# A DiT block on one core: the first modulation with the weight blocks stationary and the two condition columns moving

## The chip, the cores and the metric

The kernel runs on one core of a Trainium2 chip. The core has five engines that run side by side: TensorE (PE in the rows; its weight loads are listed apart as PEld), VectorE (DVE), ScalarE (ACT), GpSimd (POOL) and SyncE (SP, which here only issues transfers). The metric is the device time of one execution in microseconds (us); lower is better.

## What is computed

One block of a hybrid transformer: 2048 tokens of width 1024, 256 context tokens, everything in fp32. What matters here is the start, cut from the reference:

```python
mod   = silu(c)     @ w_ada + b_ada          # w_ada: 1024 x 6144
mod_c = silu(c_ctx) @ w_ada + b_ada
sh1, sc1, g1, sh2, sc2, g2 = split(mod, 6)   # six pieces of 1024
csh1, csc1, ... = split(mod_c, 6)
hx = rmsnorm(x, norm1)   * (1 + sc1)  + sh1
hc = rmsnorm(ctx, norm1) * (1 + csc1) + csh1
# then: hx and hc through w_in, gated linear attention in chunks, pooling, w_out,
# a SwiGLU with w_up and w_down, and a last norm
```

The change concerns `silu(c) @ w_ada` and `silu(c_ctx) @ w_ada` for the first two of the six pieces (columns 0 to 2047 of `w_ada`), which give `sh1`, `sc1`, `csh1` and `csc1`. Two vectors of 1024 are multiplied with a matrix of 1024 x 2048.

## The kernel before

The kernel is one function. The order of the instructions on each engine is set by a scheduler that runs over the whole program before it is built, with pools of buffers as constraints; a change in one stage can therefore move instructions in a later one. fp32 products are mostly made of three fast ones: a number is split into a rounded part in a faster fp32 format (fp32r; ScalarE copies, line 147) and the rest (VectorE subtracts, line 150), and the products high x high, high x low and low x high are summed in PSUM.

The first stage, lines 358 to 419, makes the modulation in four groups g, and does the context rows in the same loop. A group stands for 256 of the 1024 columns of `sh1` and the same of `sc1`. In a group:

- Eight blocks of `w_ada` (128 rows x 512 columns, tile `wada`, 256 KB, 12 buffers) are loaded by SP (line 365). Behind the eighth, SP loads a piece of `w_in` for the value projection (tile `xt`, line 388).
- For six of the eight, ScalarE makes the rounded part `adh` and VectorE the rest `adl` (line 373). Both are moving operands, 512 columns, of a matmul whose stationary operand is the small tile `sc4`, 128 x 4: the high and the low part of the columns c and c_ctx (lines 374 and 375). For the last two blocks, fp32 itself is the moving operand (line 369, stationary `scz`, 128 x 4).
- The result is a tile of 4 rows x 512 columns in PSUM. ScalarE copies it out (`mrow`, line 391), TensorE turns it into columns with four transposes (line 394), VectorE copies and adds the halves (`mod`, lines 396 and 397), and three short VectorE instructions make `B1` and `A1`, shift and scale by column (lines 402 to 405).
- Then `turn` gives the normed context rows, transposed by line 289, their scale and shift (`hb`, line 298 on ScalarE and 296 on VectorE), the result is split into `qh` and `ql`, the piece of `w_in` into `wvh` and `wvl` (line 407; its low part on GpSimd for the first three groups, on VectorE for the last), and 24 matmuls of 264 columns (lines 323 to 325, called from 413) add the group's share of the context's values and gates. These 24 are called the value block below.

After the four groups come the first pair of row tiles of x (transposes of line 289 again, 16 in all), the context's keys (lines 508 to 510) and then pair after pair of x.

Of the kernel before, what the change touches and what calls it, by code (L numbers as in the profile page):

```python
# [8 lines left out]
F32 = mybir.dt.float32  # L9
F32R = mybir.dt.float32r  # L10
BF16 = mybir.dt.bfloat16
AF = mybir.ActivationFunctionType
ALU = mybir.AluOpType
# [8 lines left out]
def tile_hybrid_block(ctx: ExitStack, tc: tile.TileContext, x, c, cx, c_ctx, w_ada, b_ada, norm1, w_in, conv_qk,  # L22
                      gate_bias, pool_w, pool_scale, head_norm, w_out, norm2, w_up, w_down, norm_f, out):
    nc = tc.nc
    P = 128
    T, D = x.shape[1], x.shape[2]
    TC = cx.shape[1]
    KD = D // P
# [11 lines left out]
    def pool(name, bufs=1, side="left"):  # L40
        return tc.tile_pool(name=name, bufs=bufs, side=side, reuse_waits="tile")

    def psum(name, bufs):
        return tc.tile_pool(name=name, bufs=bufs, space=PSUM, reuse_waits="tile")

    def r32(ap):
        return ap.bitcast(F32)
# [3 lines left out]
    const = cst.enter_context(tc.tile_pool(name="const", bufs=1))  # L51
# [3 lines left out]
    ident = const.tile([P, P], F32, name="ident")  # L55
# [9 lines left out]
    gbias = const.tile([P, 16], F32, name="gbias")  # L65

    scv = const.tile([P, 2, KD], F32, name="scv")
    sc4 = const.tile([P, KD, 4], F32R, name="sc4")

    scz = const.tile([P, KD, 4], F32, name="scz")  # L70
    nc.vector.memset(scz.rearrange("p k w -> p (k w)"), 0.0)
    keep = ExitStack()
    rwp = keep.enter_context(pool("rw", 3))
    vtp = keep.enter_context(pool("vt", 4))
# [2 lines left out]
    gps = pfs.enter_context(psum("gps", 1))  # L77
    tp = p1.enter_context(psum("tp", 3))
# [7 lines left out]
    pv = gps.tile([P, 512], F32, name="gps")  # L86
    nc.tensor.transpose(out=pv[:, :16], in_=crow, identity=ident[:16, :16])
    nc.vector.tensor_copy(scv.rearrange("p w k -> p (w k)"), pv[:, :16])
    scp = scv.rearrange("p w k -> p k w")
    nc.vector.tensor_copy(sc4[:, :, 0:2], scp)  # L90
    nc.vector.tensor_copy(scz[:, :, 0:2], scp)
    nc.vector.tensor_tensor(sc4[:, :, 2:4], scp, sc4[:, :, 0:2].bitcast(F32), op=ALU.subtract)

    def small_vectors():
        rows = early.tile([P, P], F32, name="rows")
        for o, n, src in ((C_BADA, 48, b_ada), (C_N1, 8, norm1), (C_N2, 8, norm2), (C_PS, 4, pool_scale),
                          (C_HN, 4, head_norm)):
            nc.scalar.dma_start(rows[o:o + n], src.rearrange("o (k p) -> (o k) p", p=P))
        nc.scalar.dma_start(rows[C_CV:C_CV + 12], conv_qk.rearrange("j (k p) -> (j k) p", p=P))
        nc.scalar.dma_start(gbias, gate_bias.to_broadcast([P, 16]))  # L100
        pv = gps.tile([P, 512], F32, name="gps")
        nc.tensor.transpose(out=pv[:, :NV], in_=rows[:NV, :], identity=ident[:NV, :NV])
        nc.vector.tensor_copy(vecs, pv[:, :NV])
# [41 lines left out]
    def split(src, hi, lo, eng_hi, eng_lo):  # L145
        if eng_hi is nc.scalar:
            nc.scalar.copy(hi, src)  # L147
        else:
            eng_hi.tensor_copy(hi, src)
        eng_lo.tensor_tensor(lo, src, r32(hi), op=ALU.subtract)  # L150
# [116 lines left out]
    def load_rows(sm, xp, src, rows):  # L267

        xs = []
        ss = sm.tile([P, 2], F32, name="ss")  # L270
        for i, r in enumerate(rows):
            xt = xp.tile([P, D], F32, name="xt")
            nc.scalar.dma_start(xt, src[r * P:(r + 1) * P, :])
            jk = sm.tile([P, D], BF16, name="jk", bufs=1)
            nc.scalar.activation(jk, xt, AF.Square, accum_out=ss[:, i:i + 1])
            xs.append(xt)
        rs = rstd_of(sm, ss, D, 2, "n")
        for i in range(2):
            nc.vector.tensor_scalar(xs[i], xs[i], rs[:, i:i + 1], None, op0=ALU.mult)
        return xs  # L280
# [54 lines left out]
    def v_store(dst, vst):  # L335
        nc.sync.dma_start(dst, vst.rearrange("p h v -> p (h v)"))

    def v_tile():
        vst = sm.tile([P, 4, 129], F32, name="vst", bufs=2)
        nc.gpsimd.memset(vst[:, :, 128:129], 1.0)  # L340
        return vst
# [16 lines left out]
    with pool("adap", 4, "right") as ap_:  # L358
        xc, turned = None, None
        for g in range(4):  # L360
            ks = range(2 * g, 2 * g + 2)
            pm = tp.tile([P, 512], F32, name="tp")[0:4, :]
            for k in range(KD):
                wt = ap_.tile([P, 512], F32, name="wada", bufs=12)
                w_last = nc.sync.dma_start(wt.rearrange("p (s c) -> p s c", s=2),
                                           w_ada[k * P:(k + 1) * P, 0:2 * D].rearrange("p (s c) -> p s c", s=2)
                                           [:, :, g * 256:(g + 1) * 256])
                if k in (6, 7):
                    nc.tensor.matmul(pm, lhsT=scz[:, k, :], rhs=wt, start=False, stop=(k == KD - 1))
                else:  # L370
                    wh = ap_.tile([P, 512], F32R, name="adh", bufs=6)
                    wl = ap_.tile([P, 512], F32R, name="adl", bufs=6)
                    split(wt, wh, wl, nc.scalar, nc.vector)
                    nc.tensor.matmul(pm, lhsT=sc4[:, k, :], rhs=wh, start=(k == 0), stop=False)
                    nc.tensor.matmul(pm, lhsT=sc4[:, k, :], rhs=wl, start=False, stop=(k == KD - 1))
                if g == 0 and k == 1:
                    small_vectors()
                    wgs = sm.tile([P, KD, 2, 8], F32, name="wgs", bufs=1)
                    nc.scalar.dma_start(wgs.rearrange("p k b g -> p k (b g)"),
                                        w_in[:, O_G:O_G + 16].rearrange("(k p) c -> p k c", p=P))  # L380
                if g == 0 and k == 3:
                    xc = load_rows(sm, xp, cx, (0, 1))
                    turned = turn(tp, "tp", xc, *hbs, A1[:, 1], B1[:, 1])
            if g == 0:
                split(wgs, wvh[:, :, :, 256:264], wvl[:, :, :, 256:264], nc.vector, nc.vector)
            st = xp.tile([P, D], F32, name="xt")
            with tc.issue_after(w_last.ins):
                nc.sync.dma_start(st.rearrange("p (k c) -> p k c", k=2),
                                  w_in[ks[0] * P:(ks[1] + 1) * P, O_V:O_V + 512].rearrange("(k p) c -> p k c", p=P))
            mrow = ap_.tile([4, 512], F32, name="mrow", bufs=2)  # L390
            nc.scalar.copy(mrow, pm)
            pt = gps.tile([P, 512], F32, name="gps")
            for m in range(4):
                nc.tensor.transpose(out=pt[:, 4 * m:4 * m + 4], in_=mrow[:, m * P:(m + 1) * P], identity=ident[0:4, 0:4])
            mod = ap_.tile([P, 4, 4], F32, name="mod", bufs=2)
            nc.vector.tensor_copy(mod.rearrange("p m w -> p (m w)"), pt[:, :16])
            nc.vector.tensor_tensor(mod[:, :, 0:2], mod[:, :, 0:2], mod[:, :, 2:4], op=ALU.add)
            kk = slice(ks[0], ks[1] + 1)

            def col(o):  # L400
                return vecs[:, None, o + ks[0]:o + ks[1] + 1].to_broadcast([P, 2, 2])
            nc.vector.tensor_tensor(B1[:, :, kk], mod[:, 0:2, 0:2].rearrange("p k w -> p w k"), col(C_BADA), op=ALU.add)
            nc.vector.tensor_tensor(A1[:, :, kk], mod[:, 2:4, 0:2].rearrange("p k w -> p w k"), col(C_BADA + 8),
                                    op=ALU.add)
            nc.vector.scalar_tensor_tensor(A1[:, :, kk], A1[:, :, kk], 1.0, col(C_N1), op0=ALU.add, op1=ALU.mult)
            next(turned)
            split(st.rearrange("p (k b c) -> p k b c", k=2, b=2), wvh[:, kk, :, 0:256], wvl[:, kk, :, 0:256],
                  nc.scalar, nc.gpsimd if g < 3 else nc.vector)
            src = hbs[g // 2][:, :, 2 * (g % 2):2 * (g % 2) + 2].rearrange("p e k c -> p k e c")
            split(src, qc[0][:, kk], qc[1][:, kk], nc.scalar, nc.vector)  # L410
            for i in range(NCC):
                for b in range(2):
                    v_mm(lambda k, e: (qc[0][:, k, e], qc[1][:, k, e]), i, b, pvs[i][b], ks)
        for i in range(NCC):
            vst = v_tile()
            for b in range(2):
                v_out(vst, b, pvs[i][b], cgat[:, i])
            v_store(s_vc[i * P:(i + 1) * P, :], vst)
# [273 lines left out]
    tp = tpp.enter_context(psum("tp1", 2))  # L692
# [474 lines left out]
    for t in range(NCH + 2):  # L1167
# [4 lines left out]
        m = t - 3  # L1172
        norm = second_norm(order[m] // 2, [X_.pop(m), X_.pop(m - 1)]) if m >= 0 and m % 2 else iter(())
        m = t - 2
# [8 lines left out]
        m = t - 1  # L1183
# [42 lines left out]
    with ExitStack() as pr:  # L1226
# [50 lines left out]
        for half in range(2):  # L1277
# [3 lines left out]
            for ff in range(NF):  # L1281
                m, fh = divmod(ff, 2)
# [9 lines left out]
                g = [tmp.tile([P, 512], F32, name=f"g{n}", bufs=2) for n in range(2)]  # L1292
# [237 lines left out]
```

## Time and profile before

| | us |
|---|---|
| time before, median of three runs | 2144.59 |
| lowest and highest of the three | 2134.82, 2145.74 |
| the profiled execution, its own time | 2133.75 |
| its span in the trace | 2132.0 |
| PE busy in the span | 2022.3 (95%) |
| DVE busy | 1411.3 (66%) |
| ACT busy | 903.2 (42%) |
| POOL busy | 231.5 (11%) |

The trace counts microseconds from the start of the span. A share of busy time is an average over the whole program; the stage of the change takes some 57 of the 2132 us, and what counts there is read from the rows of that stage. A matmul's own duration contains a fixed latency, so the rate at which TensorE works is read from the distance of the starts. An fp32 matmul whose operands are not in the faster format is listed as two rows (two passes, each with its own weight load).

### The profile page before, as it was taken

What the parts mean: (1) busy time and instruction counts of PE and PEld (TensorE: products, weight loads), DVE (VectorE), ACT (ScalarE), POOL (GpSimd) and SP (SyncE); (2) the same over time, 40 slices, a digit from 0 to 9 for tenths busy, and PEclk for the clock granted to TensorE, in tenths of its full rate; (3) what the DMA queues carried; (4) which work ended last, traced back from release to release, by engine and by line L of the source; (5) the groups of instructions that cost most, each with busy time, mean ns of one, the idle gap of its engine ahead of it and who ended that gap; (6) DMA issues with size and microseconds to landing.
All of it is one profiled execution on the core that took longest, in us unless ns stands there. A gap on an engine that the chain in (4) does not pass through costs nothing.

```text
span 2132.0 us, 27467 instructions
## 1 busy us (share of the span) xinstructions
PE 2022.3 (95%) x9482; PEld 1641.3 (77%) x9482; DVE 1411.3 (66%) x2398; ACT 903.2 (42%) x1792; POOL 231.5 (11%) x222
## 2 busy tenths in 40 slices
PE   7989999995899998999999999999999999999998
PEld 3988776674687776788888877888888788888887
DVE  6866889877365656766676578776777554447664
ACT  5644644455344544433333344333333344433442
POOL 1000123210333320000000000000000002004121
PEclk9999999996899999999999999999999999999999
DMA  8597666568477775434343267556655584644642
GB/s 278 162 291 230 204 229 197 161 184 231 136 219 238 213 220 176 148 97 147 100 141 112 96 199 249 187 188 203 188 186 194 177 325 141 221 148 157 229 162 99
DMA packets 355059, 397.80 MB, mean 187 GB/s; under 512 B 22388, under 2 KB 243160, under 8 KB 354152
## 3 DMA queue, kind: packets, MB, share of 16 engines
q1 hardware_dynamic: 308976, 324.62, 47.5%
q10 hardware_dynamic: 45944, 71.43, 10.3%
q8 instruction: 74, 1.21, 0.2%
q14 instruction: 65, 0.53, 0.1%
HBM read 269.44 MB, written 126.54 MB: 186 GB/s over the span
## 4 chain that ended last, share of the span: by engine, by line
PE 73%; DMA 11%; DVE 8%; issue 3%; ACT 3%; SPq 1%; POOL 1%; ACTq 0%; DVEq 0%; POOLq 0%
PE pa L619 8%; PE pa L620 8%; PE pa L621 8%; PE pdn L1356 7%; PE pdn L1358 7%; PE pdn L1357 7%; PE pg L619 4%; PE pg L621 4%; PE pg L620 4%; PE pb L619 2%; PE pb L621 2%; PE pb L620 2%; DMA hst<-s_hb 2%; PE pm L1138 2%; PE pm L1140 1%
## 5 line engine op out<-in xcount | busy, mean ns | idle before, releaser
L619 PE MATMUL pa<-h,wh 128*128 128x512 f32 x680 | 271.5, 400 | 8.1 <-ACT p L633 4.6
L621 PE MATMUL pa<-h,wl 128*128 128x512 f32 x680 | 270.6, 399 | 0.0
L620 PE MATMUL pa<-h,wh 128*128 128x512 f32 x680 | 270.4, 398 | 0.0
L147 ACT CAST wh<-ws 128x512 fp32r<-128x512 f32 x224 | 138.3, 620 | 299.1 <-PE pg L620 160.7
L1356 PE MATMUL pdn<-ow,op 128*128 128x512 f32 x616 | 236.8, 389 | 1.0 <-ACT op L147 1.0
L1357 PE MATMUL pdn<-ow,op 128*128 128x512 f32 x616 | 237.5, 389 | 0.0
L1358 PE MATMUL pdn<-ow,op 128*128 128x512 f32 x616 | 237.5, 389 | 0.0
L150 DVE TENSOR_TENSOR op<-ra,op 128x512 fp32r<-128x512 f32 x154 | 121.3, 794 | 156.3 <-ACT op L147 156.1
L150 DVE TENSOR_TENSOR wl<-ws,wh 128x512 fp32r<-128x512 f32 x224 | 156.7, 702 | 56.9 <-ACT wh L147 56.6
L147 ACT CAST op<-ra 128x512 fp32r<-128x512 f32 x154 | 95.2, 621 | 222.5 <-PE pdn L1358 220.0
L620 PE MATMUL pg<-h,wh 128*128 128x512 f32 x448 | 177.9, 397 | 2.4 <-DVE h L150 2.4
L619 PE MATMUL pg<-h,wh 128*128 128x512 f32 x448 | 177.5, 397 | 1.4 <-ACT h L147 1.4
L621 PE MATMUL pg<-h,wl 128*128 128x512 f32 x448 | 177.5, 396 | 1.1 <-DVE wl L150 1.1
L619 PEld LDWEIGHTS pa<-h,wh 128*128 128x128 f32 x680 | 128.9, 190 | 43.4 <-ACT p L633 6.4
L621 PEld LDWEIGHTS pa<-h,wl 128*128 128x128 f32 x680 | 128.9, 190 | 31.0 <-issue 1.2
L620 PEld LDWEIGHTS pa<-h,wh 128*128 128x128 f32 x680 | 128.9, 190 | 29.9 <-issue 0.5
L593 DVE TENSOR_TENSOR ws<-raw 128x512 f32<-128x512 f32 x110 | 78.8, 717 | 99.0 <-DMA raw<-in_w_up_dram 91.7
L1388 POOL TENSOR_TENSOR hr<-hr,o 128x1024 f32<-128x1024 f32 x8 | 21.8, 2740 | 1099.5 <-ACT o L1401 929.8
L1356 PEld LDWEIGHTS pdn<-ow,op 128*128 128x128 f32 x616 | 115.5, 188 | 25.2 <-ACT op L147 1.4
L1358 PEld LDWEIGHTS pdn<-ow,op 128*128 128x128 f32 x616 | 115.6, 188 | 24.2
L1357 PEld LDWEIGHTS pdn<-ow,op 128*128 128x128 f32 x616 | 115.6, 188 | 23.9
L1138 PE MATMUL pm<-h,mh 128*128 128x512 f32 x256 | 107.2, 419 | 7.1 <-ACT mh L147 3.7
(361 smaller groups left out, 4318.6 us busy)
## 6 DMA issues: line engine op xcount, KB each, us to landing
raw<-in_w_up_dram SPq DMA_DIRECT2D x88, 512.0 KB
ra<-s_act SPq DMA_DIRECT2D x66, 512.0 KB
s_act<-adaw SPq DMA_DIRECT2D x84, 256.0 KB
rwt<-s_t SPq DMA_DIRECT2D x77, 256.0 KB
adaw<-in_w_ada_dram SPq DMA_DIRECT2D x64, 256.0 KB
s_act<-g SPq DMA_DIRECT2D x63, 256.0 KB
raw<-in_w_in_dram SPq DMA_DIRECT2D x25, 512.0 KB
s_hb<-hb SPq DMA_DIRECT2D x7, 1792.0 KB
```

The source lines that it names most:

```text
L147: nc.scalar.copy(hi, src)
L150: eng_lo.tensor_tensor(lo, src, r32(hi), op=ALU.subtract)
L593: nc.vector.tensor_tensor(t, a, b, op=op)
L619: nc.tensor.matmul(ps, lhsT=ah[:, k], rhs=B[:, 0, k], start=st, stop=False, **kw)
L620: nc.tensor.matmul(ps, lhsT=ah[:, k], rhs=B[:, 1, k], start=False, stop=False, **kw)
L621: mm_last[0] = nc.tensor.matmul(ps, lhsT=al[:, k], rhs=B[:, 0, k], start=False, stop=(k == 3), **kw)
L1138: nc.tensor.matmul(pt, lhsT=mh[:, k], rhs=w[:, 0, k % 4], start=(k == 0), stop=False)
L1140: nc.tensor.matmul(pt, lhsT=mlo[:, k], rhs=w[:, 0, k % 4], start=False, stop=(k == 7))
L1356: nc.tensor.matmul(ps, lhsT=A[:, 0, ts_], rhs=W[:, 0], start=start, stop=False)
L1357: nc.tensor.matmul(ps, lhsT=A[:, 0, ts_], rhs=W[:, 1], start=False, stop=False)
L1358: nc.tensor.matmul(ps, lhsT=A[:, 1, ts_], rhs=W[:, 0], start=False, stop=stop)
L1388: nc.gpsimd.tensor_tensor(rows[u], rows[u], O[u][:, :, c_], op=ALU.add)
```

## The change

The blocks of `w_ada` become the stationary operand, in fp32 and as they were loaded: each 128 x 512 block is four stationary tiles of 128 x 128, and the two columns c and c_ctx (tile `scz`, now 128 x 2 for a block) are the moving operand. A block takes four fp32 matmuls with two moving columns each; the result lands in PSUM as columns, 128 x 8 for a group. The split of `w_ada` (24 copies on ScalarE, 24 subtractions on VectorE), the 48 fp32r and 8 fp32 matmuls of 512 columns, the copy of the 4 x 512 row, the 16 transposes and the addition of halves are gone. `wada` gets 16 buffers instead of 12, and the low part of the `w_in` pieces is made on VectorE in all four groups. Cut to its core:

```diff
-    sc4 = const.tile([P, KD, 4], F32R, name="sc4")
-    scz = const.tile([P, KD, 4], F32, name="scz")
+    scz = const.tile([P, KD, 2], F32, name="scz")
...
-            pm = tp.tile([P, 512], F32, name="tp")[0:4, :]
+            pt = tp.tile([P, 512], F32, name="tp")
             for k in range(KD):
-                wt = ap_.tile([P, 512], F32, name="wada", bufs=12)
+                wt = ap_.tile([P, 512], F32, name="wada", bufs=16)
...
-                if k in (6, 7):
-                    nc.tensor.matmul(pm, lhsT=scz[:, k, :], rhs=wt, start=False, stop=(k == KD - 1))
-                else:
-                    wh = ap_.tile([P, 512], F32R, name="adh", bufs=6)
-                    wl = ap_.tile([P, 512], F32R, name="adl", bufs=6)
-                    split(wt, wh, wl, nc.scalar, nc.vector)
-                    nc.tensor.matmul(pm, lhsT=sc4[:, k, :], rhs=wh, start=(k == 0), stop=False)
-                    nc.tensor.matmul(pm, lhsT=sc4[:, k, :], rhs=wl, start=False, stop=(k == KD - 1))
+                for m in range(4):
+                    nc.tensor.matmul(pt[:, 2 * m:2 * m + 2], lhsT=wt[:, m * P:(m + 1) * P], rhs=scz[:, k, :],
+                                     start=(k == 0 and m == 0), stop=(k == KD - 1), skip_group_check=True)
...
-            mrow = ap_.tile([4, 512], F32, name="mrow", bufs=2)
-            nc.scalar.copy(mrow, pm)
-            pt = gps.tile([P, 512], F32, name="gps")
-            for m in range(4):
-                nc.tensor.transpose(out=pt[:, 4 * m:4 * m + 4], in_=mrow[:, m * P:(m + 1) * P], identity=ident[0:4, 0:4])
-            mod = ap_.tile([P, 4, 4], F32, name="mod", bufs=2)
-            nc.vector.tensor_copy(mod.rearrange("p m w -> p (m w)"), pt[:, :16])
-            nc.vector.tensor_tensor(mod[:, :, 0:2], mod[:, :, 0:2], mod[:, :, 2:4], op=ALU.add)
+            mod = ap_.tile([P, 4, 2], F32, name="mod", bufs=2)
+            nc.vector.tensor_copy(mod.rearrange("p m w -> p (m w)"), pt[:, :8])
...
-                  nc.scalar, nc.gpsimd if g < 3 else nc.vector)
+                  nc.scalar, nc.vector)
```

The lines of the changed kernel have lower numbers: line 365 there is the new matmul, 283 the transpose (289 before), 317 to 319 the value block (323 to 325), 359 the load of `wada`.

The scheduler sets a new order. On TensorE, before, from the end of group 0 on: the last blocks of group 0 (lines 374, 375 and 369), the transposes of the context rows and of `mrow`, and the blocks of group 1:

```order
L374 MATMUL tp<-adh,sc_75 4x512
L375 MATMUL tp<-adl,sc_75 4x512
L369 MATMUL tp<-wada,scz 4x512 x2
L289 MATMUL tp<-ident,xt 128x128
L394 MATMUL gps<-ident,mrow 128x4 x4
L289 MATMUL tp<-ident,xt 128x128 x3
L374 MATMUL tp<-adh,sc_75 4x512
L289 MATMUL tp<-ident,xt 128x128 x4
L375 MATMUL tp<-adl,sc_75 4x512
```

And in the changed kernel, TensorE from its first matmul to the value block of group 0 (`gps<-ident,rows` turns the small vectors):

```order
L84 MATMUL gps<-ident,crow 128x16
L365 MATMUL tp<-scz,wada 128x2 x15
L96 MATMUL gps<-ident,rows 128x84
L365 MATMUL tp<-scz,wada 128x2 x17
L283 MATMUL tp<-ident,xt 128x128
L365 MATMUL tp<-scz,wada 128x2 x6
L283 MATMUL tp<-ident,xt 128x128 x3
L365 MATMUL tp<-scz,wada 128x2 x15
L317 MATMUL mm<-wvh,qh 128x264
```

Before, all 14 matmuls of group 1 stand ahead of the value block of group 0. Now 21 of the 32 of group 1 do; the other 11 follow it. Between later value blocks stand 27 (11 and 16), then 35 (16 and 19, with four transposes between), and then this, ahead of the value block of group 3, the last:

```order
L319 MATMUL mm<-wvh,ql 128x264
L365 MATMUL tp<-scz,wada 128x2 x13
L283 MATMUL tp<-ident,xt 128x128 x20
L317 MATMUL mm<-wvh,qh 128x264
L318 MATMUL mm<-wvl,qh 128x264
```

The 20 transposes are the last four of the context and all 16 of the first pair of x. Before, the first 12 of those 16 stood behind the value block of group 3, and the last four behind most of the context's keys:

```order
L323 MATMUL mm<-wvh,qh 128x264
L324 MATMUL mm<-wvl,qh 128x264
L325 MATMUL mm<-wvh,ql 128x264
L289 MATMUL tp<-ident,xt 128x128 x12
L508 MATMUL mm<-qh,vt 128x256
```

SP's order is the same over the first 108 rows. On every engine the order also differs in places up to about 400 us into the program, mostly where the pooling units run (transposed pooling products, line 750, against the products of lines 619 to 621); from there on it is the same.

## Rows read from the trace of the kernel before

**Rows 1.** Windows of the first stage: busy time of each engine, clock, DMA.

```profile
core 0: us, PE busy (x) PEld busy (x) DVE busy (x) ACT busy (x) POOL busy (x), PEclk, DMA share, GB/s
20.00:30.00 10.00, 7.96 (x28) 3.61 (x28) 8.12 (x16) 5.25 (x9) 2.16 (x2) 0.66 1.03 331
30.00:40.00 10.00, 10.00 (x57) 5.98 (x57) 8.30 (x13) 6.64 (x12) 4.11 (x4) 1.00 0.98 313
40.00:50.00 10.00, 9.92 (x58) 5.88 (x58) 8.09 (x18) 6.78 (x13) 0.23 (x4) 1.00 0.83 251
50.00:60.00 10.00, 8.59 (x73) 8.38 (x72) 8.03 (x30) 7.14 (x16) 1.51 (x3) 1.00 0.24 93
...
90.00:100.00 10.00, 10.00 (x83) 9.79 (x82) 6.56 (x17) 5.00 (x12) 0.96 (x2) 1.00 0.68 206
```

**Rows 2.** Groups by line, 0 to 50 us: busy us, mean ns, idle before.

```profile
L150 DVE TENSOR_TENSOR adl<-wada,adh 128x512 fp32r<-128x512 f32 x24 | 17.2, 755 | 0.8 <-ACT adh L147 0.8
L147 ACT CAST adh<-wada 128x512 fp32r<-128x512 f32 x24 | 13.5, 615 | 2.2 <-DMA wada<-in_w_ada_dram 1.4 <-DMA rows<-in_conv_qk_dram 0.6
```

**Rows 3.** Timeline of TensorE, first stage: start, duration, instructions, idle before and releaser.

```profile
5.60 0.59 PE L374 MATMUL tp<-adh,sc 128*4 128x512 f32 x1 [0.78 <-DVE sc L92]
...
14.57 1.02 PE L369 MATMUL tp<-wada,scz 128*4 128x512 f32 x2 [0.35 <-DMA wada<-in_w_ada_dram]
...
22.04 0.47 PE L289 MATMUL tp<-ident,xt 128*128 128x128 f32 x1 [6.45 <-DVE xt L279]
...
30.34 0.39 PE L323 MATMUL mm<-wvh,qh 128*128 128x264 f32 x1
...
35.22 0.39 PE L374 MATMUL tp<-adh,sc 128*4 128x512 f32 x1
35.45 0.40 PE L375 MATMUL tp<-adl,sc 128*4 128x512 f32 x1
...
46.11 1.88 PE L369 MATMUL tp<-wada,scz 128*4 128x512 f32 x4
...
53.05 0.39 PE L323 MATMUL mm<-wvh,qh 128*128 128x264 f32 x1 [1.41 <-ACT qh L147]
...
56.09 1.47 PE L289 MATMUL tp<-ident,xt 128*128 128x128 f32 x12
```

**Rows 4.** Timeline of TensorE's weight loads: runs of the same kind.

```profile
24.09 0.65 PEld L289 LDWEIGHTS tp<-ident,xt 128*128 128x128 f32 x3 [0.20 <-issue]
...
33.69 0.33 PEld L394 LDWEIGHTS gps<-ident,mrow 4*128 4x128 f32 x4 [0.35 <-ACT adh L147]
...
55.98 1.34 PEld L289 LDWEIGHTS tp<-ident,xt 128*128 128x128 f32 x12
...
793.82 1.99 PEld L1081 LDWEIGHTS po<-vt,raw 128*128 128x128 f32 x16
```

**Rows 5.** Timeline of TensorE: the value block after a long wait, and later.

```profile
128.71 0.59 PE L323 MATMUL mm<-wvh,qh 128*128 128x264 f32 x1 [5.65 <-ACT qh L147]
129.09 0.42 PE L324 MATMUL mm<-wvl,qh 128*128 128x264 f32 x1
129.31 0.42 PE L323 MATMUL mm<-wvh,qh 128*128 128x264 f32 x1
...
133.07 0.28 PE L324 MATMUL mm<-wvl,qh 128*128 128x264 f32 x1
133.19 0.28 PE L325 MATMUL mm<-wvh,ql 128*128 128x264 f32 x1
```

**Rows 6.** Window of a stretch of short matmuls, columns as in Rows 1.

```profile
488.75:492.16 3.41, 3.04 (x13) 2.45 (x13) 1.71 (x3) 1.67 (x5) 0.00 (x0) 0.50 0.79 194
```

**Rows 7.** Timeline of VectorE: the norm's scaling, beside GpSimd's split and alone.

```profile
19.10 3.55 DVE L279 TENSOR_SCALAR xt<-xt,nrs 128x1024 f32<-128x1024 f32 x2 [0.83 <-DMA wada<-in_w_ada_dram]
...
56.31 1.42 DVE L279 TENSOR_SCALAR xt<-xt,nrs 128x1024 f32<-128x1024 f32 x2 [0.48 <-POOL nrs L142]
```

**Rows 8.** Windows of 260 to 420 us, their sum: columns as in Rows 1.

```profile
sum 160.00, PE 147.30 PEld 109.48 DVE 141.31 ACT 74.05 POOL 40.41; mean PE 18.41 PEld 13.69 DVE 17.66 ACT 9.26 POOL 5.05
```

More of the change, by code (lines that the diff above doesn't have):

```diff
@@ L67, in tile_hybrid_block @@
     scv = const.tile([P, 2, KD], F32, name="scv")
-    sc4 = const.tile([P, KD, 4], F32R, name="sc4")
-    scz = const.tile([P, KD, 4], F32, name="scz")
-    nc.vector.memset(scz.rearrange("p k w -> p (k w)"), 0.0)
+    scz = const.tile([P, KD, 2], F32, name="scz")
     keep = ExitStack()
@@ L88, in tile_hybrid_block @@
     nc.vector.tensor_copy(scv.rearrange("p w k -> p (w k)"), pv[:, :16])
[L89 to L92, printed above, removed]
+    nc.vector.tensor_copy(scz, scv.rearrange("p w k -> p k w"))
     def small_vectors():
```

## The prediction, made before the changed kernel was run

> **What bounds the kernel now.** I read first the windows of the first stage [rows 1]. From 30 to 50 us TensorE is busy all the time, VectorE 8.1 to 8.3 us in ten, ScalarE under 7, and the transfers 98% and then 83%. So in the second half of the stage TensorE is late, and what the change gives VectorE and ScalarE back is no gain by itself. Then the timeline [rows 3]: the modulation's matmuls begin at 5.60, group 0's last ones run at 14.57, behind a transfer, and TensorE then waits 6.45 us for the normed context rows (22.04). From there to the end of group 3's last matmuls (46.11 + 1.88 = 47.99) it waits little; it waits 1.41 us for group 3's `qh` (53.05), ends the last value block at 56.09 and then has 12 of the 16 transposes of the first pair of x, which end at 57.3 (starts 0.105 us apart, below). With the other four I put the end of what both kernels must have done by then at **57.7**. Behind it TensorE stays the late one (busy 8.6 us in ten from 50 to 60 and all ten from 90 to 100 [rows 1]), so a later end of the stage is a later end of the program, nearly one to one.
>
> **Removed work.** VectorE loses 24 subtractions, 17.2 us, and ScalarE 24 copies, 13.5 us [rows 2], and four copies of `mrow`. On the path these count where they make TensorE late: GpSimd's split of `w_in` slows VectorE (two scalings took 3.55 us beside it and 1.42 without it [rows 7]), and with that split moved to VectorE, where 17.2 us came free, the context rows are ready some 2 us earlier. TensorE loses 48 matmuls with starts 0.23 us apart (35.22, 35.45 [rows 3]) at the high clock, 11.1 us, and 16 passes of fp32 at (1.88 - 0.59) / 3 = 0.43, 6.9 us, and 16 transposes of `mrow` at (0.33 - 0.13) / 3 = 0.066, 1.1 us [rows 4] (0.13 taken as one load's duration): 19 us in all.
>
> **Added work.** 4 groups x 8 blocks x 4 tiles = 128 fp32 matmuls, two passes each: **256 passes**, each with a weight load of 128 columns for two moving columns. No row of before shows that. The nearest rows are runs of weight loads [rows 4]. From below: `mrow`'s transposes with four moving columns, 0.066 us a pass, but as transposes they load in another mode. From above at the high clock: line 1081, 128 x 128 weights in the faster format and 129 moving columns, (1.99 - 0.19) / 15 = 0.12; the transposes of x with 128 columns, (1.34 - 0.19) / 11 = 0.105. I take 0.12, the row with a plain 128 x 128 load, since two columns instead of 129 shorten the matmul but not the load. 256 x 0.12 = 31 us against 19, on the engine that is late; the bounds are 17 and 31 at the high clock.
>
> At the low clock it is about twice that. The value block's matmuls after a wait of 5.65 us have starts 0.22 apart (129.09, 129.31), and 4 us later 0.12 (133.07, 133.19) [rows 5]; a transpose at 24.09, in the window whose granted clock is 0.66 [rows 1], takes (0.65 - 0.23) / 2 = 0.21, 0.23 being taken as one load [rows 4]. A pass at the low clock I put at 0.213, so 256 would be 55 us.
>
> **Which clock.** That is the open term, since matmuls with two columns leave the array almost idle while TensorE is busy loading. The nearest rows are a stretch of short matmuls of 129 columns with a weight load each: TensorE busy 3.04 of 3.41 us and loading 2.45, and the granted clock is 0.50, the lower level (1.2 GHz) [rows 6]. So being busy with loads and short matmuls did not raise the clock there; with two columns there is less still. I take the low clock for the start, up to and including the first value block, and behind it a mixture, because each value block is dense.
>
> **The sum, along the new order of TensorE** (the order's pieces are in the section on the change):
> - Group 0's 64 passes from 5.60 at 0.213: 13.6, to 19.2. The blocks arrive faster than that.
> - Four transposes at 0.21 and 42 passes of group 1: 0.8 + 8.9, to 28.9. The chain from the modulation to `qh` (copy, A1, B1, scale, split: about 5 us from 19.2) lies under it.
> - Value block 0, 24 x 0.22 = 5.3: 34.2. Before, it began at 30.34 [rows 3].
> - What is left up to the 57.7 mark: 22 + 32 + 70 + 26 = 150 passes, 28 transposes, three value blocks of 24. High clock: 18.0 + 2.9 + 8.7 = 29.6, to 63.8, which is +6.1. Low clock: 32.0 + 5.9 + 15.8 = 53.7, to 87.9, which is +30.2.
> - I take a fifth of the way between them, +4.8: the three stretches of passes are 6 to 8 us at the high clock, each behind a dense block, and I expect their later parts at the low clock. +10.9.
> - Given back behind the mark: the wait of 1.41 us for the last `qh` is now covered by 20 transposes, and ScalarE and VectorE go on without a backlog. That is worth at most the idle time of TensorE there, 1.4 us of the ten from 50 to 60 [rows 1] and, estimated, half as much later: -2.
>
> So **+9 us**. The later reordering (up to 400 us, around line 750) I cost at nothing with a width of 3 either way: TensorE idles 160 - 147.3 = 12.7 us in 260 to 420 [rows 8], the work there is the same, and a quarter of that is a large shift. 16 buffers instead of 12 are nothing: TensorE lags, and the transfers of group 3 have until after 45 us.
>
> The sum stands against the profiled execution: 2133.75 + 9 = 2143. That run was 10.8 us under the median of the three. On the median 2144.59 the same +9 is **2154**.
>
> **Rivals.**
> *The clock stays low for the whole stage.* For it: the 0.50 row [rows 6], and stretches of 54 and 70 passes between dense blocks of 24 matmuls. Against it: the value blocks alone are 24 dense matmuls, and 4 us of such raised the pace [rows 5]. It gives +15 to +30, 2160 to 2175: slower. It decides when over half of the 150 later passes run at starts of 0.2.
> The Trainium skill ("TensorE: Matmul & The Clock Gate", Part 1, "What's actually happening") says that the throttled state is the default and that activity releases it; rows 5 agree. Its Part 4 says that transposes do not count as busy in the same way, which no stretch here shows alone; if weight loads count as little, this rival is the outcome.
>
> *The clock is high from early on.* Loads count as work, group 0 is done soon after its last block (about 16), value block 0 begins near 25 (context rows ready at 20.5 instead of 22, then the chain), 2.9 + 29.6 more and a short wait for the last `qh`: 58 to 59, less the 2 given back. -3 to +3, 2142 to 2148: no change. Against it rows 6.
>
> *The passes are cheap and TensorE is no longer late.* At 0.066 a pass, the 150 passes take 9.9, the rest from 28 on 21.5, the mark is reached near 50; with a wait for `qh`, -6, with the freed engines up to -12: 2133 to 2139. Against it: line 1081's 0.12, and that its load is a plain one. The skill's same page ("Back-to-back issue gap") gives about 60 cycles for a matmul of 1 to 64 columns, 25 ns. By it alone 256 passes would be 6.4 us, the transfers would end the stage, and the gain would be about that of this rival; the rows of loads, 0.066 to 0.12, say that the load sets the pace.
>
> *It does not do what it says* would need the scheduler to put the freed time elsewhere on the path; the order shows the value blocks later and not earlier, so I fold it into the second rival.
>
> **How the numbers follow.** 0.5% of 2144.59 is 10.7 us; less than that a measurement of this kernel cannot tell from no change, since three runs spread over 10.9. Forecast (+4 to +15, centre +9): 0.45, of which 0.15 lies over 10.7. Low clock throughout: 0.18. High clock: 0.27. Cheap passes: 0.10, of which 0.05 lies beyond -10.7. So slower 0.33, same 0.30 + 0.27 + 0.05 = 0.62, faster 0.05. The range takes the high-clock rival in with the runs' spread below it, and the lower two thirds of the low-clock rival: 2137 to 2169. Outside are most of the cheap passes and the worst of the low clock, under 0.2.
>
> **What would show it.** In the changed profile: 256 rows of loads for the new line, 128 columns each. Starts 0.2 apart before the first value block and a granted clock of 0.5 there show the first steps right; 0.12 throughout and a clock of 1.0 show the high-clock rival; under 0.07 the cheap one. Value block 0 should begin near 29 and the 20 transposes should end near 65 to 70 with the last value block behind. ScalarE and VectorE should be half idle up to 45. It is wrong if TensorE waits for `wada` in groups 2 and 3, or if the difference between the two traces arises after 260 us and not before 80.

## The result, and the profile after

The changed kernel took **2157.03 us** (median of 10 runs, 2151.36 to 2164.07); the kernel before 2141.74 (10 runs, 2134.82 to 2148.06). The ratio is **1.0078, 95% interval [1.0059, 1.0097]**: slower by 0.78%, 17 us (the ratio is of the means of the runs; the medians lie 15.3 us apart). A second comparison (after_copy, below) gave 1.0084 [1.0060, 1.0108].

The profiled execution of the changed kernel took 2161.51 us, with a span of 2159.7 and a mean granted clock of 0.966 (before: 2132.0 and 0.975). Windows of its first 80 us, columns as in [rows 1]:

```profile
0.00:10.00 10.00, 5.04 (x24) 4.96 (x24) 1.02 (x8) 1.59 (x2) 1.05 (x12) 1.00 0.69 191
10.00:20.00 10.00, 10.00 (x50) 10.00 (x49) 3.96 (x11) 3.34 (x5) 0.71 (x1) 1.00 1.06 364
20.00:30.00 10.00, 10.00 (x48) 10.00 (x49) 2.37 (x3) 2.13 (x3) 0.00 (x0) 1.00 1.09 359
30.00:40.00 10.00, 10.00 (x64) 10.00 (x62) 3.02 (x7) 2.23 (x3) 0.00 (x0) 0.80 0.84 264
40.00:50.00 10.00, 10.00 (x62) 10.00 (x61) 2.60 (x4) 4.39 (x7) 0.00 (x0) 0.67 0.68 202
50.00:60.00 10.00, 10.00 (x49) 10.00 (x49) 3.31 (x9) 1.18 (x2) 0.71 (x1) 0.50 0.00 1
60.00:70.00 10.00, 10.00 (x62) 10.00 (x62) 0.35 (x3) 0.00 (x0) 0.00 (x0) 0.67 0.01 2
70.00:80.00 10.00, 9.45 (x65) 8.84 (x63) 7.64 (x23) 8.41 (x18) 1.00 (x1) 0.83 0.66 249
```

Against [rows 1]: TensorE is busy without a gap from 10 to 70 us, and its weight loads (the second pair of columns) are as busy as it is, where before they were busy 3.6 to 6.0 us in ten from 20 to 50. There VectorE falls from over 8 us in ten to 2.4 to 3.0, ScalarE from 5.2 to 6.8 to 2.1 to 4.4, and from 50 to 70 us hardly any bytes move. TensorE alone is late. From 50 to 60 us its granted clock is 0.50, the lower level (1.2 GHz).

The new line, 365, over the whole run (durations min/median/max in ns), and the stage's timeline of TensorE (line 283 transposes x, line 493 is the keys' product, the first work behind the last value block):

```profile
L365 PEld LDWEIGHTS tp<-scz,wada x256: 188/333/370, 5.2 to 69.3; 128*128 128x128 f32 x128
L365 PE MATMUL tp<-scz,wada x256: 166/352/374, 5.2 to 69.3; 128*128 128x2 f32 x128
```

```profile
5.22 6.56 PE L365 MATMUL tp<-scz,wada 128*128 128x2 f32 x30 [0.48 <-DVE scz L86]
11.81 7.33 PE L365 MATMUL tp<-scz,wada 128*128 128x2 f32 x34
...
19.25 2.56 PE L365 MATMUL tp<-scz,wada 128*128 128x2 f32 x12
...
22.34 6.40 PE L365 MATMUL tp<-scz,wada 128*128 128x2 f32 x30
...
33.36 2.51 PE L365 MATMUL tp<-scz,wada 128*128 128x2 f32 x22
35.73 0.93 PE L283 MATMUL tp<-ident,xt 128*128 128x128 f32 x4
36.45 6.83 PE L365 MATMUL tp<-scz,wada 128*128 128x2 f32 x32
...
47.51 4.93 PE L365 MATMUL tp<-scz,wada 128*128 128x2 f32 x32
52.30 1.09 PE L283 MATMUL tp<-ident,xt 128*128 128x128 f32 x4
53.19 8.11 PE L365 MATMUL tp<-scz,wada 128*128 128x2 f32 x38
...
66.58 3.00 PE L365 MATMUL tp<-scz,wada 128*128 128x2 f32 x26
69.44 4.17 PE L283 MATMUL tp<-ident,xt 128*128 128x128 f32 x20
...
73.57 0.29 PE L318 MATMUL mm<-wvl,qh 128*128 128x264 f32 x1
73.69 0.28 PE L317 MATMUL mm<-wvh,qh 128*128 128x264 f32 x1
...
77.07 0.36 PE L493 MATMUL mm<-qh,vt 128*128 128x256 f32 x1 [0.56 <-DVE cgat L327]
```

A run's duration holds the length of its last pass, about 0.35 at the slow pace and 0.17 at the fast one. So the passes start (6.56 - 0.35) / 29 = 0.214 us apart in the first run, and 0.213 in the second. Behind value block 0, which ends at 33.36, 22 passes start (2.51 - 0.17) / 21 = 0.11 apart, then 32 again (6.83 - 0.35) / 31 = 0.21, and behind block 2, 26 start 0.11 apart. These are the two paces that the prediction worked with, 0.213 and 0.12, and nothing between them. The 32 behind block 1 hold both: by the length of their run, (4.93 - 0.35) us for 31 starts, about 20 started 0.11 apart and 11 started 0.213 apart.

How far each kernel is, from the first start of a line in its trace (us; the copies are second profiles of the same kernels):

| kernel | value block 0 | keys | first unit | first pool matmul to first K/V product | first unit to the last stage |
|---|---|---|---|---|---|
| before | 30.3 | 57.3 | 180.8 | 119.2 | 1524.2 |
| before_copy | 29.2 | 56.2 | 178.9 | 119.7 | 1536.9 |
| after | 28.6 | 77.1 | 199.8 | 126.9 | 1533.0 |
| after_copy | 28.5 | 76.6 | 200.1 | 127.1 | 1527.3 |
| a_gps | 28.5 | 76.7 | 200.1 | 127.7 | 1525.4 |
| c16 | 28.4 | 73.0 | 199.6 | 126.9 | 1529.6 |
| c64 | 28.4 | 63.8 | 186.7 | 126.6 | 1530.1 |
| c128 | 29.1 | 61.2 | 183.5 | 130.0 | 1529.9 |
| c128_8 | 24.6 | 61.5 | 184.7 | 122.9 | 1520.6 |
| half | 26.8 | 56.5 | 182.0 | 122.6 | 1520.6 |
| b_dve | 29.4 | 54.3 | 175.9 | 118.9 | 1532.5 |
| bd8 | 31.0 | 59.6 | 181.6 | 120.5 | 1524.8 |
| b_16 | 30.9 | 59.8 | 181.7 | 125.2 | 1531.3 |
| g0v | 25.3 | 59.6 | 186.8 | 119.2 | 1527.4 |

"First unit" is the first product of line 619 (604 after), the work behind the first stage and the value projection; the last stage, from the first to the last start of its line 1356 (before), takes 418.3 to 418.4 us in all of them. The whole of the loss is there by 77 us: +19.8 at the keys, and +19.0 at the first unit (+20.1 between the means of the two profiles each).

### The profile page after: what moved, and what is told of

Same layout as the page of the kernel before. It is cut to its first block, busy times and chain, and to the rows that moved or that the text cites. A ratio compares the mean times of both kernels' runs of the same rounds, so it can differ in the third digit from the quotient of the medians.

```text
span 2159.7 us, 27712 instructions
## 1 busy us (share of the span) xinstructions
PE 2047.0 (95%) x9658; PEld 1692.1 (78%) x9658; DVE 1396.2 (65%) x2370; ACT 888.7 (41%) x1764; POOL 226.4 (10%) x219
## 4 chain that ended last, share of the span: by engine, by line
PE 63%; DMA 8%; DVE 5%; issue 2%; ACT 1%; SPq 1%; POOL 1%; ACTq 0%; DVEq 0%; POOLq 0%
PE pa L606 7%; PE pa L605 7%; PE pa L604 7%; PE pdn L1341 6%; PE pdn L1342 6%; PE pdn L1343 6%; PE pg L606 3%; PE pg L605 3%; PE pg L604 3%; PE pb L604 2%; PE pb L605 2%; PE pb L606 2%; PE pm L1123 2%; PE pm L1125 2%; PE pm L1124 2%
## 5 line engine op out<-in xcount | busy, mean ns | idle before, releaser
L144 DVE TENSOR_TENSOR wl<-ws,wh 128x512 fp32r<-128x512 f32 x224 | 159.4, 714 | 53.7 <-ACT wh L141 53.5
L605 PEld LDWEIGHTS pa<-h,wh 128*128 128x128 f32 x680 | 129.2, 190 | 29.4 <-issue 0.7
L606 PEld LDWEIGHTS pa<-h,wl 128*128 128x128 f32 x680 | 129.0, 190 | 28.9 <-issue 1.0
```

The costliest lines, as they stand in the source:

```text
L605: nc.tensor.matmul(ps, lhsT=ah[:, k], rhs=B[:, 1, k], start=False, stop=False, **kw)
L606: mm_last[0] = nc.tensor.matmul(ps, lhsT=al[:, k], rhs=B[:, 0, k], start=False, stop=(k == 3), **kw)
```

## Experiments

The theory: the loads set the pace, one load takes 0.11 at the high clock and 0.213 at the low one, and matmuls with two moving columns let the clock fall back, so most passes are slow. The rivals: the load takes what it takes at any clock, or the passes are not what is late.

### More moving columns: c16, c64, c128

The two columns are repeated by a broadcast, so a pass has the same load and 16, 64 or 128 moving columns; `mod` copies two of each tile's. For 128:

```
-  nc.tensor.matmul(pt[:, 2 * m:2 * m + 2], lhsT=wt[:, m * P:(m + 1) * P], rhs=scz[:, k, :],
+  nc.tensor.matmul(pt[:, 128 * m:128 * (m + 1)].rearrange("p (r w) -> p r w", w=2),
+                   lhsT=wt[:, m * P:(m + 1) * P], rhs=scz[:, k, None, :].to_broadcast([P, 64, 2]),
```

> The same with 16 moving columns. Theory: the array is still idle most of the time, so the clock stays low: starts of 0.2, last value block within 4 us of 77, ratio to before 1.006 to 1.010. Rival (any cost that goes with a matmul of very few columns, not the clock): 16 columns would already be faster, 0.12 apart.

> Moving operand of 64 columns (the two columns repeated 32 times) instead of 2; weight loads, their number and the arithmetic that is used stay. Theory (the passes are slow because the array is nearly idle in them and the clock stays at its low level): starts of the passes drop from 0.21 to about 0.12 us at least behind the value blocks, the last value block ends at 60 to 70 us instead of 77.1, time 5 to 15 us under the changed kernel, ratio to before 1.001 to 1.005. Rival (an fp32 weight load costs 0.21 us here at any clock): starts stay at 0.21, the last value block ends at 77 or later, ratio to before 1.007 to 1.010.

> The same with 128 moving columns, as many as the transposes of x stream. Theory: the array works about all the time, the clock goes up within the first group, passes 0.11 to 0.12 apart, last value block ends at 57 to 63 us, ratio to before 0.999 to 1.003. Rival: starts 0.21 or more since the columns come on top, last value block at 77 to 90 us, ratio 1.008 to 1.015.

Measured against before: c16 2155.08 us, 1.0095 [1.0071, 1.0118]; c64 2141.01, 1.0037 [1.0020, 1.0054]; c128 2136.82, 1.0011 [0.9995, 1.0027]. The ratios are those of the theory in all three; c16's keys, at 73.0, come 4.1 us before 77.1, at the edge of the 4 us that were given. The timelines of TensorE behind value block 0, of c16, c64 and c128:

```profile
36.26 10.26 PE L365 MATMUL tp<-scz,wada 128*128 128x16 f32 x48
```

```profile
36.42 5.47 PE L365 MATMUL tp<-scz,wada 128*128 128x64 f32 x48
```

```profile
32.12 7.53 PE L365 MATMUL tp<-scz,wada 128*128 128x128 f32 x66
```

The same 48 passes take 10.26 us with 16 columns (0.21 apart) and 5.47 with 64 (0.11 apart). Up to these 48 the two kernels have the same order. A pass with thirty times the moving columns of the changed kernel's is half as long. The clock column of c64 agrees, and its windows of the same stretch have half again as many matmuls as those of the changed kernel:

```profile
40.00:50.00 10.00, 10.00 (x90) 10.00 (x89) 3.06 (x8) 4.39 (x7) 0.06 (x1) 1.00 0.64 186
50.00:60.00 10.00, 9.07 (x77) 8.65 (x77) 4.21 (x11) 2.85 (x6) 0.65 (x1) 1.00 0.11 26
```

So the load is not slow in itself, the clock is: behind block 0 it fell back with 2 and with 16 columns and stayed up with 64. Of the 150 passes there, 81 start 0.18 us apart or more with 2 columns, 59 with 16 and one with 64 (counted from the starts in the traces). Of the 19 us, 13 go with 64 columns and 16 with 128 (first unit at 186.7 and 183.5). In c64 the first 106 passes, ahead of value block 0, are still 0.22 apart (first fence); with 128 columns the pace rose there too (second fence: the first 30 passes are 0.17 apart in the mean, the next ten 0.11), and TensorE then waited for blocks of `wada` (2.42 us at 15.51).

```profile
5.01 6.66 PE L365 MATMUL tp<-scz,wada 128*128 128x64 f32 x30 [0.47 <-DVE scz L86]
```

```profile
5.25 5.18 PE L365 MATMUL tp<-scz,wada 128*128 128x128 f32 x30 [0.48 <-DVE scz L86]
...
10.34 1.31 PE L365 MATMUL tp<-scz,wada 128*128 128x128 f32 x10
```

What is left in c128, 3 us at the first unit, fits the work at the high clock, 256 x 0.11 = 28 us against the 19 removed, part of it under waits; no run takes it apart. Against b_dve below, which shares the change's other part, c128 is 7.6 us later there.

### Half the passes: half

Two of the four tiles of each block are multiplied and stand for the other two, so half of the modulation is left out.

```
-                for m in range(4):
+                for m in range(2):
```

> Half of the new matmuls left out (two of the four tiles of each block, 128 passes less; the scale columns are then wrong). Theory: the passes are the cost on the path, so the last value block ends 10 to 20 us before 77.1, ratio to before 0.998 to 1.003. Rival (the passes are hidden, and the late value blocks or the new order cost the time): the last value block moves by under 4 us and the ratio stays above 1.006.

Measured 2131.79 us, 0.9984 [0.9968, 1.0000]; first unit at 182.0. 128 passes fewer took 17.8 us off the stage, 0.14 each, and most loads are still slow (median 333 ns, as in the changed kernel). The passes are what was late. But even with half of them the first unit is not earlier than in the kernel before.

### The change's other part: b_dve, and a_gps without it

b_dve is the kernel before with the low split of `w_in` on VectorE, as in the change; a_gps is the changed kernel with that split on GpSimd again.

```
-                  nc.scalar, nc.gpsimd if g < 3 else nc.vector)
+                  nc.scalar, nc.vector)
```

> The kernel before with the low split of w_in's value columns moved from GpSimd to VectorE for groups 0 to 2, nothing else: the change's other part alone. Theory 'GpSimd slows VectorE, but TensorE is the late engine': unit start within 1 us of 180.8, total 0 +- 2. Rival 'VectorE feeds the late chain': VectorE has three more splits of 512 columns, about 0.7 us each, among work that is 83% busy: +2 to +4. Other rival: context rows and normed rows come 2 us earlier: -2 to -4.

> The changed kernel with its second part undone: the low split of w_in's value columns for groups 0 to 2 is on GpSimd again. The later order stays that of the changed kernel. b_dve showed this part alone as worth 0.27% and a first stage 4.9 us shorter where VectorE is late. Theory 'in the changed kernel TensorE's passes end the stage': VectorE is half idle there, so unit start moves by under 2 us from 199.8 and the total by 0 +- 3 against the changed kernel. Rival 'the split's part is worth the same in both': unit start 204 to 205, total +5 to +6 more, ratio to before near 1.0105.

b_dve: 2129.75 us, **0.9973 [0.9960, 0.9985]**; it is faster than both kernels. In its timeline the first transpose of the context rows starts at 19.17 after a wait of 2.15, in the kernel before at 22.04 after 6.45 [rows 3], and in the second profile of that kernel (second fence) at 20.78:

```profile
19.17 0.33 PE L289 MATMUL tp<-ident,xt 128*128 128x128 f32 x1 [2.15 <-DVE xt L279]
```

```profile
20.78 0.48 PE L289 MATMUL tp<-ident,xt 128*128 128x128 f32 x1 [4.09 <-DVE xt L279]
```

The two scalings of `xt` took 1.42 us in b_dve and 3.55 in [rows 7], where GpSimd's split ran beside them. The first unit comes 3.0 to 4.9 us earlier. So the second rival of its expectation held, and more than it said (the interval is -3 to -9 us), and TensorE was not the only late engine of the kernel before: it waited for VectorE here. How the shorter scalings become the gain is not shown. The order changed with them (among others, four more transposes of the context rows stand ahead of value block 0, which starts at 29.4, no earlier than the 29.2 of before_copy), and the lead appears by the keys, with the wait of 1.41 us for group 3's `qh` [rows 3] gone as well. The scalings take 1.42 us in g0v and bd8 below too, and those two gain nothing.

a_gps: 2154.68 us, 1.0100 [1.0074, 1.0127], first unit at 200.1 against 199.8 and 200.1. As expected: in the changed kernel no gain of this part can be seen; TensorE, busy throughout, covers it. What gained some 6 us beside the old modulation is thus hidden under the change's own loss.

### Group 0 alone in the new form: g0v

b_dve with group 0's eight blocks in the new form (128 moving columns), groups 1 to 3 in the old one.

```
+                if g == 0:
+                    for m in range(4):
+                        nc.tensor.matmul(pm4[:, 128 * m:128 * (m + 1)].rearrange("p (r w) -> p r w", w=2),
+                                         lhsT=wt[:, m * P:(m + 1) * P],
+                                         rhs=scz[:, k, None, 0:2].to_broadcast([P, 64, 2]),
...
```

> The kernel before with only group 0's modulation in the new form (128 moving columns, 64 passes), groups 1 to 3 as before, and the low split of w_in on VectorE for all groups. TensorE waits 6.45 us for the context rows in group 0, so 64 passes at 0.11 to 0.21 (7 to 14 us from 5.6 on) lie under transfers and that wait; 12 passes of the old form and their splits go. Theory 'the passes cost only where TensorE is late': value block 0 starts 1 to 2 us earlier than 30.3, the stage ends 1 to 4 us earlier, the later order is that of before, total -1 to -4. Rival 'the low clock is carried over': group 1's matmuls run at half pace for some us more, total +2 to +6.

Measured 2137.28 us, 1.0012 [0.9998, 1.0026]: no gain. Value block 0 did start 5 us earlier (25.3), and group 0's passes cost nothing. But the order behind it changed too: TensorE then waited 2.80 us for `xt` at 51.36, the value matmuls behind that wait start 0.22 apart, it waited 3.5 us for the gates (line 333), and the first unit is at 186.8, 10.9 later than in b_dve. Which of these comes first was not separated. "The low clock is carried over" held in size (+6 at the first unit; in all about +2.5, where +2 to +6 were expected), but not where it was expected.

### Buffers and the later order: b_16, c128_8, bd8

The number of `wada` buffers alone also moves the scheduler's order, up to the pool units: 16 in the kernel before (b_16), 8 in c128 (c128_8), 8 in b_dve (bd8).

```
-                wt = ap_.tile([P, 512], F32, name="wada", bufs=12)
+                wt = ap_.tile([P, 512], F32, name="wada", bufs=16)
```

> The kernel before with one number changed: 16 buffers for `wada` instead of 12. The arithmetic is that of before; the scheduler's order changes from the first stage up to the end of the pool units, where it becomes that of the changed kernel (after the last pool matmul the `pb` products follow at once, where before five `pg` products stood between). Theory 'the later order costs': from the start of the first unit to the first K/V column product the time rises from 119.2 us (before) to 124-127, and the total by 4 to 8, with a first stage as before (unit start 180.8 +- 1). Rival 'the lateness costs' (the extra 7.7 us of the changed kernel come from its late first stage): 119 us, total 0 +- 2.

> c128 (128 moving columns) with 8 `wada` buffers instead of 16. The scheduler's order in the pool units then is another one, that of the kernel with half the passes. Theory 'the later order costs': from unit start to the first K/V column product 122-124 us instead of 130.0, unit start near 183 as in c128, total 2136.8 - 6 = 2131. Rival 'the lateness costs': near 130, total 2137. If eight buffers starve TensorE, the unit start goes up by 2 to 5 us: total 2139-2142.

> b_dve with 8 buffers for `wada` instead of 12, which gives the later order of before once more (119 us in the pool stretch). Theory 'VectorE is what b_dve relieves': unit start 176 to 178, total -4 to -7 against before. If eight buffers hold transfers back: unit start 179 to 182, total -2 to +1.

The question behind them was a second difference between the two traces, from 323 us on: between the first pool matmul and the first K/V column product the changed kernel takes 126.9 us and the kernel before 119.2. At its end (first fence before, second after; pool matmul lines 750 and 735, first `pb` product lines 619 and 604):

```profile
398.56 1.12 PE L750 MATMUL tp<-pd,pw 128*128 128x512 f32 x2 [0.24 <-DVE pd L782]
...
404.61 0.50 PE L619 MATMUL pb<-h,vt 128*128 128x512 f32 x1 [3.30 <-DVE pre L713]
```

```profile
422.87 1.10 PE L735 MATMUL tp<-pd,pw 128*128 128x512 f32 x2 [2.12 <-DVE pd L767]
...
431.61 0.79 PE L604 MATMUL pb<-h,vt 128*128 128x512 f32 x1 [7.18 <-DVE pre L698]
```

And VectorE of the changed kernel there:

```profile
430.87 0.69 DVE L698 TENSOR_TENSOR pre<-pb,p 128x512 f32<-128x512 f32 x1 [5.71 <-DMA s_pm<-pd]
```

The `pb` product waits for VectorE, and VectorE for the last pool result to reach memory (the last fence), since `pre` takes over the pool's buffers. Before, five `pg` products filled part of that wait; in the new order they have run earlier. This wait is 3.9 us longer than before. Over the whole stretch TensorE waits 16.7 us and before 10.1; the other 2.7 us are waits for `u` and `h` ahead of the last pool matmul.

b_16 took 2143.3 us, 1.0037 [1.0021, 1.0054], with 125.2 us in that stretch and the first unit 0.9 later: as the order theory said, +8 us from a buffer count. Its profile does not show where they arise: from the first unit to the last stage it takes 1531.3 us, within what the profiles of the other orders take. c128_8 took 2133.9, 1.0003 [0.9988, 1.0018], with 122.9 instead of 130.0: the stretch as expected, but against before only 0.08% (2 us) better than c128, where 6 us were expected; the first unit is 1.2 later. bd8 missed its main expectation: 2137.46, 1.0008 [0.9994, 1.0021], first unit at 181.6, so with eight buffers b_dve's gain is gone; that was the expectation's second case.

### Second profiles: after_copy, before_copy

> The changed kernel itself, for a second profile and a second comparison. Theory 'the order sets the stretch from the first pool matmul to the first K/V column product': 126.9 us again within 0.5, while the stretch from there to the last stage (1282.4 us in the first profile) moves by several us; ratio to before 1.008 +- 0.002. Rival 'one run's chance': 119 to 130 in that stretch.

> The kernel before itself, for a second profile. Theory 'the order sets it': 119.2 us within 0.5 from the first pool matmul to the first K/V column product, unit start 180.8 within 1; the stretch from there to the last stage 1281.5 us within some us. Rival 'one run's chance': over 122 in that stretch.

after_copy: 2152.81 us, 1.0084 [1.0060, 1.0108]; before_copy: 2137.65, 1.0006 [0.9988, 1.0024]. The pool stretch repeats to 0.5 us (127.1 and 119.7; a_gps, c16 and c64 with the same order there: 127.7, 126.9, 126.6). So it is the order's, and not chance. But the table's last column says that it is not a loss of the whole: from the first unit to the last stage the five profiles with the changed kernel's later order (after, after_copy, a_gps, c16, c64) take 1525.4 to 1533.0, mean 1529.1, and the five with the order of before in the pool stretch (before, before_copy, b_dve, bd8, g0v) 1524.2 to 1536.9, mean 1529.2. The 7.7 us are given back elsewhere on the way, in amounts that differ by several us from one execution to the next; where, these runs do not settle.

## Why the prediction was right and where it was wrong

The time, 2154.0, was 3.0 us from the measured 2157.03, inside the range, and the sign of the forecast held. But part of that nearness is the reference: the median of before that the +9 was added to, 2144.59, was 2.9 above the one measured beside the changed kernel, and that is luck. The loss is 17 us and not 9, over the 0.5% mark, on the side that had been given 0.33 and not on that given 0.62.

**What bounds the kernel** held for the stage as a whole: TensorE's end moved the program's end nearly one to one (+20 at the first unit, +17 in the time). It was incomplete at one place: b_dve shows that VectorE's part was worth 6 us by itself.

**Up to value block 0** the steps held closely. Group 0's 64 passes were put at 5.60 to 19.2 and took 5.22 to 19.0; block 0 was put at 28.9 to 34.2 and stood at 28.6 to 33.36. The load as the price, 0.213 at the low clock and 0.12 at the high, measured 0.213 and 0.11. The granted clock of 0.5 that was to go with the slow starts cannot be read there: the clock column says 1.00 up to 30 us. The rival of cheap passes falls: no pass took 0.066, which transposes of four columns had shown [rows 4].

The Trainium skill ("TensorE: Matmul & The Clock Gate", "Back-to-back issue gap") gives about 25 ns for a matmul of 1 to 64 columns, and says that in a stream of loads and matmuls both set the spacing. The runs agree with the second: with a fresh 128 x 128 fp32 load for each, starts are 110 ns apart at best.

**The step that failed is the fifth of the way.** Behind block 0 the sum put 150 passes, 28 transposes and three value blocks at 29.6 us (high clock) to 53.7 (low clock) and took +4.8, 34.4 us. They took 77.07 - 33.36 = 43.7, which is (43.7 - 29.6) / 24.1 = 0.58 of the way, and all three terms shared in it. The passes, by starts, took 24.7 (20.8 in the sum), the value blocks 13.6 (10.1), the transposes 5.4 (3.5). Only 69 of the 150 passes ran at the fast pace, and 81 at the slow one (the runs of 32 and 38, and 11 of the 32 behind block 1): the reason that had been given, a dense block ahead of each stretch, raised the clock for the first 20 to 26 passes, and behind that it was down again. With the pace down, blocks 0 and 1 began at the slow pace and block 2 ran at it whole: the granted clock is 0.50 in the 8 us of passes ahead of it and in the block.

```profile
53.00:61.00 8.00, 8.00 (x40) 8.00 (x38) 1.35 (x3) 1.18 (x2) 0.00 (x0) 0.50 0.00 1
61.00:66.50 5.50, 5.50 (x26) 5.50 (x26) 0.00 (x0) 0.00 (x0) 0.00 (x0) 0.50 0.00 0
```

The row for it had been there: [rows 6], loads and short matmuls at 0.50. It was used for the start alone. The low-clock rival, "over half of the later passes at starts of 0.2" and +15 to +30, was nearer to the truth than the forecast: by that sign, 81 of 150, it came true, and the stage's +20 lies in its range. A sign that the prediction gave for itself failed with it: the 20 transposes end at 73.3 and not near 65 to 70.

The Trainium skill ("TensorE: Matmul & The Clock Gate", Part 4) says that transposes do not count as busy in the same way. From it the prediction asked whether loads count as little; c16 against c64 shows that they did not keep the clock up, with loads equally busy and the pace 0.21 and 0.11. For transposes the trace of the changed kernel has one stretch that speaks against the rule: from 70.2 to 73.3 us TensorE did nothing but transposes (with one wait of 0.37 us), at the slow pace, and then the clock rose, since block 3 starts 0.12 apart from 73.57 on. The 8 us of passes from 53.2 on were followed by no such rise.

**The 2 us given back** did not come: the lead of before at the keys, 19.8 us, is still 19.0 at the first unit. The wait for `qh` that bounds a later block is the same in both kernels, only 19 us later (5.65 us at 128.71 in [rows 5]):

```profile
PE mm L317 <- ACT qh L141: 5.6, 1, 5.6
```

**The later reordering**, put at 0 with 3 either way, was 0.1 between the means of five profiles each. That it would do nothing was wrong: it costs 7.7 us in the pool stretch and they come back elsewhere. Within each five the profiles lie 8 to 13 us apart, so a few us either way stay open; and b_16, 8 us slower from a buffer count, speaks for more width than 3.

**VectorE and ScalarE** are half idle up to 45 us, as foreseen, and TensorE never waited for `wada`.

## What to carry to other kernels

Making a block of weights the stationary operand for two moving columns turns a product into weight loads, and in this stage TensorE was as busy with them as with its matmuls: count loads, at the pace of the clock that such work gets. If few columns are all there is to move, look for the clock that rows of short matmuls got in the same trace and price the whole stretch with it too, not its start alone; here the truth lay 0.58 of the way to that price. Repeating the columns bought back 16 of 19 us here, but not the loads themselves. When a change has several parts, price each alone: the one that gained here with 12 buffers (a split taken off GpSimd) was hidden by the one that lost.

## What the runs showed of the hardware that was not expected

- More moving columns made a pass shorter. For the same 128 x 128 fp32 load, the passes behind value block 0 fell back to starts 0.21 us apart with 2 columns (81 of 150) and with 16 (59), and stayed at 0.11 with 64. Loads busy all the time did not hold the clock up.
- The weight load follows the clock: 188 ns at the shortest and 333 at the median in the changed kernel, with starts 0.11 and 0.213 apart.
- The clock column of the windows reads 1.00 from 10 to 30 us, where passes start 0.213 apart, the pace that later goes with 0.50. There the pace is the better witness; behind 36 us the two agree.
- Two scalings of 128 x 1024 on VectorE took 3.55 us beside GpSimd's split (before, before_copy, b_16) and 1.42 without it (b_dve, g0v, bd8).
- Twelve buffers or sixteen, with the same arithmetic, made 8 us of difference (b_16); the order of instructions up to some 400 us is what changed with them.
